# RWKV columns: where a pair's scores and its turned b and k stand, and the row count of two lo products

## The chip, the cores and the metric

The kernel runs on one core of a Trainium2 chip. A core has a matrix engine (TensorE, PE in the profile, with its weight loads as PEld), VectorE (DVE), ScalarE (ACT), GpSimd (POOL), a queue engine that issues transfers (SP), and 16 DMA engines. Each engine executes its own instructions in the order of its program. Matrix products go to PSUM, which has eight banks of 128 x 512 float32. The metric is the time of one execution on the device in microseconds, lower is better.

## The reference, cut to what matters

One decoder layer on a sequence of 1024 tokens with 1024 channels. The part in question is the RWKV-7 branch: 8 heads of 64 channels, whose projections of the normalised input are shifted by one token, turned into decay, rate a, key k, removal vector kk, receptance r and value v, and scanned along the sequence.

```python
p_rwkv = p_rwkv + mu_shift[l] * (prev - p_rwkv)
r, wd, k, v, ad, gd = _split(p, RWKV_COLS)
w = -jax.nn.softplus(-(decay_base + jnp.tanh(wd) @ w_decay_up)) - 0.5
decay = jnp.exp(-jnp.exp(w))
a = jax.nn.sigmoid(iclr_base + ad @ w_iclr_up)
kk = heads(k * kk_scale)                      # then divided by its norm over the head
k = heads(k * (1.0 + (a - 1.0) * k_iclr_mix))
a_vec, b_vec = -kk, kk * a_h
def step(state, inp):                         # 1024 steps
    r_t, w_t, k_t, v_t, a_t, b_t = inp
    sa = jnp.einsum('bhij,bhj->bhi', state, a_t)
    state = state * w_t[:, :, None, :] + sa[..., None] * b_t[:, :, None, :] + v_t[..., None] * k_t[:, :, None, :]
    return state, jnp.einsum('bhij,bhj->bhi', state, r_t)
```

The other branch is forgetting attention (8 heads, softmax with a cumulative bias made from forget gates). Both are merged by gates, projected and added to the residual, and a squared-ReLU MLP follows.

## The kernel before, in words

The scan is done in 16 chunks of 64 tokens. Inside a chunk every pair of tokens needs a score, the product of (kk, r) of one with (b, k) of the other, each scaled by its decay. The stage of the RWKV columns, some 200 us long, makes all of this before the attention and the chunk chain start. It runs over four pairs of heads (`for p in range(4)`, L509), 128 channels per pair on the 128 partitions, tokens along the free axis. For each pair, in the order of writing:

- *Decay and rate* (L511 to L521). Two low-rank products per half of the tokens: p_dec and p_icl, each a product with the high part of the up weights on 128 rows and one with their low part (lo) on 64 rows. The moving operand x2 holds the high part of the 64 inner channels in one half of its rows and the low part in the other, and the weights are loaded twice, one copy in each half. ScalarE makes the tanh (L520, L521). VectorE then makes the step, its running sum (L526), and ScalarE two exponentials ee and ei (L530, L532). wcs (L533) holds a chunk's whole decay.
- *k* (L536 to L552): a projection of 48 matmuls of 128 x 512 (three products of split operands, 8 row blocks, 2 halves), the token shift (`shifted`, L448 on ScalarE and L449 on VectorE), and from it the kk half of the tile ar and both halves of the tile bk, which holds b and k. head_sums (L496) sums kk squared over each head.
- *r* (L555 to L561): projection, shift, the r half of ar (L558), the bonus (L559) and its head sums (tile bo, emptied by ScalarE at L506), the store of ar.
- *v* (L564 to L573): projection, shift, eight transposes (vp) and a store.
- *Scores* (L576 to L586): four groups of four chunks. A group is 16 matmuls on 64 rows each into two PSUM banks, two masked copies on VectorE (COPY_PREDICATED, L585) into one of two score buffers scb, and a 512 KB store to sc_d. The copy must wait until the store of two groups before has landed.
- *Turned b and k* (L589 to L596): one VectorE product of all of bk with wcs, then four times four transposes (bp, L593), a ScalarE copy into one of two staging buffers (tag bt), and a 256 KB store to bk_d.

After the loop come loads of the two sums, the attention's forget-gate bias (`fox_bias`, tile p_f, 32 matmuls and a chain of small VectorE operations), the transposes of those sums, and the gate projection (p_gd). Then the attention starts on TensorE, while GpSimd inverts the chunks' triangular matrices (`inverse`), whose result w_d is read by the chunk chain (`chain`).

What sets the order: the code above gives only data flow and an order of writing. The framework's planner makes each engine's program from it with its own costs for every operation. It takes, among what it holds to be ready, what is written first, so that written-later work fills the waits that it foresees (in the trace matmuls of the next k projection stand between those of v and the scores). On the chip the order is fixed, and an engine waits at its next instruction whatever stands behind it. Small PSUM tiles (`bank`) share four banks, which are handed out in turn; projections (`big`) share two double banks. Most SBUF tiles of the stage have one buffer per name, among them bk, ar, kt and th, so that the next pair's tile needs the last reader of this one. Weights of a projection are loaded two projections ahead on the SP queue, which also issues all stores of the stage.

The functions that the change touches:

Of the kernel before, what the change touches and what calls it, by code (L numbers as in the profile page):

```python
# [8 lines left out]
F32 = mybir.dt.float32  # L9
# [26 lines left out]
def build(ctx, tc, A, out):  # L36
# [3 lines left out]
    def mm(o, l, r, start, stop):  # L40
        PE.matmul(o, l, r, start=start, stop=stop)  # L41
# [24 lines left out]
    def bank(name, tag="ps"):  # L66
        return big(name, tag)
# [96 lines left out]
    def load_w(src, k0, nk, name, to=wp):  # L164

        raw = to.tile([P, nk, P], F32, tag="wraw", name=f"wr_{name}", bufs=2)
        if isinstance(src, (list, tuple)):
            o = 0
            for s_ in src:
                w_ = s_.shape[2]  # L170
                SP.dma_start(raw[:, :, o : o + w_], s_)
                o += w_
        else:
            SP.dma_start(raw, src)
        hi = to.tile([P, nk, P], F32R, tag="whi", name=f"wh_{name}", bufs=2)
        lo = to.tile([P, nk, P], F32R, tag="wlo", name=f"wl_{name}", bufs=2)
        ACT.copy(hi, raw)
        DVE.tensor_tensor(lo, raw, hi.bitcast(F32), ALU.subtract)  # L178
        return hi, lo
# [3 lines left out]
    def win(c0, n=P):  # L183
        return w_in[:, :, c0 : c0 + n]
# [153 lines left out]
    def proj(w, name, ahi=hhi, alo=hlo):  # L338
        hi, lo = w
        o = big(name)  # L340
        for hf in range(2):
            sl = slice(hf * 512, hf * 512 + 512)
            for k in range(KT):
                mm(o[:, sl], hi[:, k, :], ahi[:, k, sl], k == 0, False)
                mm(o[:, sl], lo[:, k, :], ahi[:, k, sl], False, False)
                mm(o[:, sl], hi[:, k, :], alo[:, k, sl], False, k == KT - 1)
        return o
# [111 lines left out]
    with pool(name="ra", bufs=1) as ra:  # L459
# [31 lines left out]
            xs2.append(x2)  # L491

        v4 = lambda ap: ap.rearrange("p (c t) -> p c t", t=C)
        nsc = 0

        def head_sums(a, name, dst, n):  # L496

            hi, lo = [ra.tile([P, S], F32R, name=f"{name}{x}", tag=f"hs{x}") for x in "hl"]
# [7 lines left out]
                ACT.copy(a[0:2, sl], o[0:2])  # L506
            SP.dma_start(dst.rearrange("g h n -> h g n"), a[0:2].rearrange("h (g n) -> h g n", n=n))

        for p in range(4):  # L509

            th = ra.tile([P, S], F32, tag="th", name=f"th{p}")  # L511
            tha = ra.tile([P, S], F32, tag="tha", name=f"tha{p}")
            for hf in range(2):
                sl = slice(hf * 512, hf * 512 + 512)
                od, oi = bank(f"p_dec{p}_{hf}"), bank(f"p_icl{p}_{hf}")
                for i, o in ((0, od), (1, oi)):
                    (hi, lo), me = ups2[i], slice(64 * i, 64 * i + 64)
                    mm(o, hi[:, p * P : (p + 1) * P], xs2[i][:, sl], True, False)
                    mm(o, lo[me, p * P : (p + 1) * P], xs2[i][me, sl], False, True)
                ACT.activation(th[:, sl], od, AF.Tanh, bias=hbase[:, p : p + 1], scale=0.5)  # L520
                ACT.activation(tha[:, sl], oi, AF.Tanh, bias=hbase[:, 4 + p : 5 + p], scale=0.5)  # L521
            stp = step[p % 2]
            DVE.tensor_scalar(stp[:, :, 1:], v4(th), 0.5, 0.5, ALU.mult, ALU.add)
            lc = ra.tile([P, NCH, C + 1], F32, tag="lc", name=f"lc{p}")
            flat = lambda t_: t_.rearrange("p c t -> p (c t)")
            DVE.tensor_tensor_scan(flat(lc), flat(reset), flat(stp), 0.0, ALU.mult, ALU.add)  # L526
            lx = ra.tile([P, NCH, C + 1], F32, tag="lx", name=f"lx{p}")
            DVE.tensor_tensor(lx, lc, lc[:, :, C // 2 : C // 2 + 1].broadcast_to([P, NCH, C + 1]), ALU.subtract)
            ee = ra.tile([P, NCH, C + 1], F32, tag="ee", name=f"ee{p}")
            ACT.activation(ee, lx, AF.Exp, scale=-KAPPA)  # L530
            ei = ra.tile([P, NCH, C + 1], F32, tag="ei", name=f"ei{p}")
            ACT.activation(ei, lx, AF.Exp, scale=KAPPA)  # L532
            DVE.tensor_tensor(wcs[:, p, 0 : NCH - 1].unsqueeze(2), ee[:, 0 : NCH - 1, C : C + 1], ei[:, 1:NCH, 0:1], ALU.mult)  # L533


            o = proj(load_w(win(COL_K + p * P), 0, KT, f"k{p}"), f"p_k{p}") if p else firsts[2][1]  # L536
            kt_ = ra.tile([P, S], F32, tag="kt", name=f"kt{p}")
            shifted(o, 1 + p, kt_)
            ar = ra.tile([P, NCH, P], F32, tag="ar", name=f"ar{p}")
            bk = ra.tile([P, NCH, P], F32, tag="bk", name=f"bk{p}")  # L540
            kks = vcol("kks", p)
            kk2 = ra.tile([P, S], F32, tag="vk", name=f"kk2{p}")
            ACT.activation(kk2, kt_, AF.Square, scale=kks)
            head_sums(kk2, f"sq{p}", sq_d[:, 2 * p : 2 * p + 2], C)
            DVE.scalar_tensor_tensor(ar[:, :, 0:64], v4(kt_), kks, ee[:, :, 0:C], ALU.mult, ALU.mult)
            at = ra.tile([P, S], F32, tag="at", name=f"at{p}")
            (DVE if p else POOL).tensor_scalar(at, tha, 0.5, 0.5, ALU.mult, ALU.add)
            DVE.scalar_tensor_tensor(at, kt_, kks, at, ALU.mult, ALU.mult)
            DVE.tensor_tensor(bk[:, :, 0:64], v4(at), ei[:, :, 1:], ALU.mult)
            (DVE if p else POOL).tensor_scalar(tha, tha, kmh[:, p : p + 1], kmo[:, p : p + 1], ALU.mult, ALU.add)  # L550
            DVE.tensor_tensor(kt_, kt_, tha, ALU.mult)
            DVE.tensor_tensor(bk[:, :, 64:128], v4(kt_), ei[:, :, 1:], ALU.mult)  # L552


            o = proj(load_w(win(COL_R + p * P), 0, KT, f"r{p}"), f"p_r{p}") if p else firsts[1][1]  # L555
            rt = ra.tile([P, S], F32, tag="rt", name=f"rt{p}")
            shifted(o, 5 + p, rt)
            DVE.tensor_tensor(ar[:, :, 64:128], v4(rt), ee[:, :, 1:], ALU.mult)  # L558
            DVE.scalar_tensor_tensor(rt, rt, vcol("rb", p), kt_, ALU.mult, ALU.mult)  # L559
            head_sums(rt, f"bo{p}", bo_d[:, 2 * p : 2 * p + 2], P)  # L560
            SP.dma_start(ar_d.rearrange("c q p n -> q c p n")[:, :, p, :], ar)  # L561


            o = proj(load_w(win(COL_V + p * P), 0, KT, f"v{p}"), f"p_v{p}")  # L564
            vt_ = ra.tile([P, S], F32, tag="vt", name=f"vt{p}")
            shifted(o, 9 + p, vt_)
            vk = ra.tile([P, 8, P], F32, tag="vk", name=f"vk{p}")
            for g in range(2):
                vp = bank(f"vp{p}_{g}")
                for t in range(4):  # L570
                    PE.transpose(vp[:, t * P : (t + 1) * P], vt_[:, (4 * g + t) * P : (4 * g + t + 1) * P], ident)
                ACT.copy(vk[:, 4 * g : 4 * g + 4, :], vp.rearrange("p (t n) -> p t n", n=P))
            SP.dma_start(v_d.rearrange("(t q) n -> q t n", q=P)[:, :, p * P : (p + 1) * P], vk)  # L573


            for g in range(4):  # L576
                sp_ = [bank(f"sc{p}_{g}_{hh}").rearrange("p (c n) -> p c n", c=4) for hh in range(2)]
                for c in range(4):
                    for hh in range(2):
                        hs = slice(64 * hh, 64 * hh + 64)  # L580
                        mm(sp_[hh][:, c, :], bk[hs, 4 * g + c, :], ar[hs, 4 * g + c, :], True, True)
                sb = scb[nsc % 2]
                nsc += 1
                for hh in range(2):
                    DVE.copy_predicated(sb[:, :, hh, :], mask.unsqueeze(1).broadcast_to([P, 4, P]), sp_[hh])  # L585
                SP.dma_start(sc_d[:, 4 * g : 4 * g + 4, p, :], sb.rearrange("p c h n -> p c (h n)"))  # L586


            DVE.tensor_tensor(bk, bk, wcs[:, p, :].unsqueeze(2).broadcast_to([P, NCH, P]), ALU.mult)  # L589
            for g in range(4):  # L590
                bp = bank(f"bp{p}_{g}")
                for c in range(4):
                    PE.transpose(bp[:, c * P : (c + 1) * P], bk[:, 4 * g + c, :], ident)  # L593
                bt = ra.tile([P, 4, P], F32, tag="bt", name=f"bt{p}_{g}", bufs=2)
                ACT.copy(bt, bp.rearrange("p (c n) -> p c n", n=P))
                SP.dma_start(bk_d.rearrange("c q p n -> q c p n")[:, 4 * g : 4 * g + 4, p, :], bt)  # L596

        bol = ra.tile([64, P], F32, name="bol", tag="bt", bufs=2)
        SP.dma_start(nri, sq_d.rearrange("c h s -> (c h) s"))
        SP.dma_start(bol, bo_d.rearrange("t h s -> (t h) s"))  # L600
        fox_bias(ra)
        DVE.tensor_scalar(nri, nri, 1e-24, -1.0, ALU.max, ALU.mult)
        DVE.reciprocal(nri, nri)
        hp = bank("nrp")
# [1053 lines left out]
```

## Time and profile before

| | us |
|---|---|
| median of 3 runs | 1693.91 (1693.02 to 1697.69) |
| profiled execution | 1695.53 |
| its span, first to last instruction | 1693.8 |
| TensorE busy | 1603.3 (95%), mean granted clock 0.988 |
| VectorE, ScalarE, GpSimd busy | 1131.1, 731.3, 359.5 |
| the RWKV columns, from the pairs' first products to the gate projection | about 90 to 289 |

Times in the profile count from the span's start. A matmul's duration is longer than the distance to the next start, since matmuls are pipelined: a stream of 128 x 512 products has 0.39 us each and starts 0.23 us apart. So costs on TensorE are read from the distances between starts. A number in brackets behind a row is the idle time of the engine before it and who ended it. The granted clock is 1.00 at 2.4 GHz and lower in stretches where part of the time ran at 1.2 GHz.

### The profile page before, as it was taken

Reading aid. Unit: us, or ns where it says so; the run is one execution under the profiler, and the core shown is the slowest. Engines: PE = TensorE matmul, PEld = TensorE weight load, DVE = VectorE, ACT = ScalarE, POOL = GpSimd, SP = SyncE. Lnnn points to the kernel's source line nnn. Section 1 sums busy time; section 2 is a strip of 40 time slices with the busy share of each in tenths; the row PEclk is TensorE's granted clock in tenths of the full one; section 3 lists DMA queues with packets and bytes.
Section 4 is the critical chain, followed back from the end, with each engine's and each line's share of the span. In section 5 each row is a group of like instructions: output and inputs, shape, how many; then the busy total and the mean of one; then the engine's idle time right before and its main releaser. Section 6 shows DMA issues by size and latency. Waiting matters only on the chain.

```text
span 1693.8 us, 21902 instructions
## 1 busy us (share of the span) xinstructions
PE 1603.3 (95%) x8293; PEld 1277.2 (75%) x8293; DVE 1131.1 (67%) x1685; ACT 731.3 (43%) x1138; POOL 359.5 (21%) x362
## 2 busy tenths in 40 slices
PE   2999998998999999999999999999999979999997
PEld 2767766776777878888887787777777858888886
DVE  5677665556665736667647655975555579799878
ACT  5454432444454723332233334655555534333334
POOL 4310000699992011121110000112211110000000
PEclk9999999999999999999999999999999989999999
DMA  8534433622223167778768421344444474354422
GB/s 247 140 100 150 127 111 122 155 55 69 61 80 107 44 186 251 224 228 247 230 212 245 171 100 63 131 152 151 146 160 156 164 271 174 124 205 161 157 75 100
DMA packets 217111, 256.24 MB, mean 151 GB/s; under 512 B 30097, under 2 KB 156330, under 8 KB 216878
## 3 DMA queue, kind: packets, MB, share of 16 engines
q1 hardware_dynamic: 204094, 209.99, 40.5%
q0 software_dynamic: 12704, 44.57, 6.9%
q8 instruction: 65, 1.06, 0.3%
q14 instruction: 40, 0.33, 0.1%
q10 hardware_dynamic: 208, 0.28, 0.0%
HBM read 178.16 MB, written 72.45 MB: 148 GB/s over the span
## 4 chain that ended last, share of the span: by engine, by line
PE 71%; DVE 9%; DMA 7%; ACT 3%; issue 2%; SPq 1%; POOL 0%; DVEq 0%; ACTq 0%
PE x L1215 18%; PE y L1215 11%; PE p_out L41 5%; PE p_gb L41 4%; PE p_ga L41 3%; PE p_fk L41 3%; PE p_fq L41 2%; PE my L41 2%; PE p_fv L41 2%; PE p_ob L41 2%; DMA ur<-in_w_ff 2%; PE yv L41 2%; PE p_v L41 2%; PE z L1215 2%; PE p_r L41 2%
## 5 line engine op out<-in xcount | busy, mean ns | idle before, releaser
L1404 ACT CAST dh<-dA 128x1024 fp32r<-128x1024 f32 x54 | 56.4, 1046 | 143.8 <-PE x L1215 74.5
L1215 PE MATMUL x<-wh,dh 128*128 128x512 f32 x256 | 103.7, 405 | 9.4 <-ACT wh L1093 9.4
L1215 PE MATMUL x<-wh,fl 128*128 128x512 f32 x256 | 101.3, 396 | 0.0
L639 POOL TENSOR_TENSOR dg<-dg,inv 128x62 f32<-128x62 f32 (+30 forms) x62 | 100.2, 1615 | 4.8
L1215 PE MATMUL x<-wl,dh 128*128 128x512 f32 x256 | 101.1, 396 | 0.0
L638 POOL TENSOR_TENSOR inv<-dg 128x62 f32<-128x62 f32 (+30 forms) x62 | 92.9, 1498 | 4.9
L1585 DVE TENSOR_TENSOR fl<-dA,dh 128x1024 fp32r<-128x1024 f32 x54 | 65.3, 1218 | 19.4 <-ACT dh L1404 13.1
L1215 PE MATMUL y<-wh,dh 128*128 128x512 f32 x176 | 70.3, 400 | 0.0
L1215 PE MATMUL y<-wl,dh 128*128 128x512 f32 x176 | 68.8, 394 | 0.6 <-DVE wl L1094 0.6
L1215 PE MATMUL y<-wh,fl 128*128 128x512 f32 x176 | 69.2, 393 | 0.0
L823 DVE TENSOR_TENSOR pl<-tp,ph 128x512 fp32r<-128x512 f32 (+1 forms) x80 | 49.1, 631 | 24.7 <-ACT ph L822 24.4
L1215 PEld LDWEIGHTS x<-wh,dh 128*128 128x128 f32 x256 | 48.7, 190 | 20.9 <-ACT wh L1093 9.8
L879 DVE CUSTOM_DVE_ANT_0 pt<-s,cb 128x512 f32<-128x512 f32 (+2 forms) x64 | 36.3, 584 | 37.0 <-PE s L41 36.4
L881 ACT ACTIVATE pt<-pt,sm 128x128 f32<-128x128 f32 (+3 forms) x64 | 49.5, 775 | 25.4 <-DVE sm L879 24.4
L1239 ACT ACTIVATE ff<-ff 128x512 f32<-128x512 f32 x48 | 30.3, 632 | 64.8 <-DVE ff L1325 29.4
L1215 PEld LDWEIGHTS x<-wl,dh 128*128 128x128 f32 x256 | 48.4, 189 | 13.1 <-DVE wl L1094 0.5
L701 POOL TENSOR_TENSOR sw<-sbd,wcs 64x256 f32<-64x256 f32 x28 | 21.9, 782 | 171.3 <-DVE sbd L702 139.3
L1215 PEld LDWEIGHTS x<-wh,fl 128*128 128x128 f32 x256 | 48.6, 190 | 11.4
L822 ACT CAST ph<-tp 128x512 fp32r<-128x512 f32 (+1 forms) x80 | 41.4, 543 | 28.5 <-PE tp L819 26.9
L1230 POOL DMA_DIRECT2D f_d<-ff x48 | 26.0, 542 | 123.5 <-ACT ff L1240 119.0
L41 PE MATMUL p_out<-h_wo,hhi 128*128 128x512 f32 x128 | 50.8, 396 | 1.1 <-ACT h_wo L1050 1.1
L41 PE MATMUL p_gb<-hhi,wl_gb 128*128 128x512 f32 x128 | 51.5, 402 | 0.2 <-DVE wl_gb L178 0.2
(586 smaller groups left out, 4938.1 us busy)
## 6 DMA issues: line engine op xcount, KB each, us to landing
dA<-f_d SPq DMA_DIRECT2D x27, 1024.0 KB
aw<-in_w_ada SPq DMA_DIRECT2D x32, 512.0 KB
ur<-in_w_ff SPq DMA_DIRECT2D x30, 512.0 KB
B<-in_w_ff SPq DMA_DIRECT2D x15, 1024.0 KB
f_d<-ff POOLq DMA_DIRECT2D x48, 256.0 KB, 4.4
wa<-in_w_ada SPq DMA_DIRECT2D x16, 512.0 KB
sc_d<-scb SPq DMA_DIRECT2D x16, 512.0 KB
sct<-sc_d SPq DMA_DIRECT2D x16, 512.0 KB
```

Source lines behind the costliest of these rows:

```text
L41: PE.matmul(o, l, r, start=start, stop=stop)
L638: POOL.tensor_tensor(tv, dg[:, 0:s, s : s + 1].broadcast_to([P, s, m]), dg[:, s : s + 1, s + 1 :].broadcast_to([P, s, m]), ALU.mult)
L639: POOL.tensor_tensor(dg[:, 0:s, s + 1 :], dg[:, 0:s, s + 1 :], tv, ALU.add)
L822: ACT.copy(ph[:, 0:w_], tp[:, 0:w_])
L823: DVE.tensor_tensor(pl[:, 0:w_], tp[:, 0:w_], ph[:, 0:w_].bitcast(F32), ALU.subtract)
L879: DVE.tensor_tensor_reduce(pt[:, c0:c1], sv, cb[:, c0:c1], -0.125, low, ALU.add, ALU.min, st_[:, x : x + 1])
L881: ACT.activation(pt[:, 0:n], pt[:, 0:n], AF.Exp, bias=low, scale=-1.0, accum_out=ls[:, b : b + 1])
L1215: PE.matmul(o, l, r, start=start, stop=stop, skip_group_check=True)
L1230: POOL.dma_start(f_d[AOPS.index(name), j], src)
L1239: ACT.activation(f, f, AF.Relu)
L1404: ACT.copy(hs[i], src[:, 2 * i : 2 * i + 2])
L1585: DVE.tensor_tensor(fl[:, sl], src[:, sl], f32(hs[i_]), ALU.subtract)
```

## The change

The loop body of scores becomes a function `scores(p, bk, ar, gs)` and the turning of b and k a function `leave(p, bk)`. Groups 0 and 1 of a pair's scores are now written ahead of v's projection, groups 2 and 3 where all four were. The turning of a pair's b and k is written behind the next pair's k projection, and for the last pair behind `fox_bias`. The lo products of decay and rate run on all 128 rows of weights and x2; this adds the product of the low weights with the low part of x.

```diff
--- before.py
+++ after.py
@@ -491,8 +491,6 @@
             xs2.append(x2)
 
         v4 = lambda ap: ap.rearrange("p (c t) -> p c t", t=C)
-        nsc = 0
-
         def head_sums(a, name, dst, n):
 
             hi, lo = [ra.tile([P, S], F32R, name=f"{name}{x}", tag=f"hs{x}") for x in "hl"]
@@ -506,6 +504,30 @@
                 ACT.copy(a[0:2, sl], o[0:2])
             SP.dma_start(dst.rearrange("g h n -> h g n"), a[0:2].rearrange("h (g n) -> h g n", n=n))
 
+        def scores(p, bk, ar, gs):
+
+            for g in gs:
+                sp_ = [bank(f"sc{p}_{g}_{hh}").rearrange("p (c n) -> p c n", c=4) for hh in range(2)]
+                for c in range(4):
+                    for hh in range(2):
+                        hs = slice(64 * hh, 64 * hh + 64)
+                        mm(sp_[hh][:, c, :], bk[hs, 4 * g + c, :], ar[hs, 4 * g + c, :], True, True)
+                sb = scb[g % 2]
+                for hh in range(2):
+                    DVE.copy_predicated(sb[:, :, hh, :], mask.unsqueeze(1).broadcast_to([P, 4, P]), sp_[hh])
+                SP.dma_start(sc_d[:, 4 * g : 4 * g + 4, p, :], sb.rearrange("p c h n -> p c (h n)"))
+
+        def leave(p, bk):
+
+            DVE.tensor_tensor(bk, bk, wcs[:, p, :].unsqueeze(2).broadcast_to([P, NCH, P]), ALU.mult)
+            for g in range(4):
+                bp = bank(f"bp{p}_{g}")
+                for c in range(4):
+                    PE.transpose(bp[:, c * P : (c + 1) * P], bk[:, 4 * g + c, :], ident)
+                bt = ra.tile([P, 4, P], F32, tag="bt", name=f"bt{p}_{g}", bufs=2)
+                ACT.copy(bt, bp.rearrange("p (c n) -> p c n", n=P))
+                SP.dma_start(bk_d.rearrange("c q p n -> q c p n")[:, 4 * g : 4 * g + 4, p, :], bt)
+
         for p in range(4):
 
             th = ra.tile([P, S], F32, tag="th", name=f"th{p}")
@@ -514,9 +536,9 @@
                 sl = slice(hf * 512, hf * 512 + 512)
                 od, oi = bank(f"p_dec{p}_{hf}"), bank(f"p_icl{p}_{hf}")
                 for i, o in ((0, od), (1, oi)):
-                    (hi, lo), me = ups2[i], slice(64 * i, 64 * i + 64)
+                    hi, lo = ups2[i]
                     mm(o, hi[:, p * P : (p + 1) * P], xs2[i][:, sl], True, False)
-                    mm(o, lo[me, p * P : (p + 1) * P], xs2[i][me, sl], False, True)
+                    mm(o, lo[:, p * P : (p + 1) * P], xs2[i][:, sl], False, True)
                 ACT.activation(th[:, sl], od, AF.Tanh, bias=hbase[:, p : p + 1], scale=0.5)
                 ACT.activation(tha[:, sl], oi, AF.Tanh, bias=hbase[:, 4 + p : 5 + p], scale=0.5)
             stp = step[p % 2]
@@ -534,6 +556,8 @@
 
 
             o = proj(load_w(win(COL_K + p * P), 0, KT, f"k{p}"), f"p_k{p}") if p else firsts[2][1]
+            if p:
+                leave(p - 1, bk)
             kt_ = ra.tile([P, S], F32, tag="kt", name=f"kt{p}")
             shifted(o, 1 + p, kt_)
             ar = ra.tile([P, NCH, P], F32, tag="ar", name=f"ar{p}")
@@ -560,6 +584,8 @@
             head_sums(rt, f"bo{p}", bo_d[:, 2 * p : 2 * p + 2], P)
             SP.dma_start(ar_d.rearrange("c q p n -> q c p n")[:, :, p, :], ar)
 
+            scores(p, bk, ar, (0, 1))
+
 
             o = proj(load_w(win(COL_V + p * P), 0, KT, f"v{p}"), f"p_v{p}")
             vt_ = ra.tile([P, S], F32, tag="vt", name=f"vt{p}")
@@ -572,33 +598,13 @@
                 ACT.copy(vk[:, 4 * g : 4 * g + 4, :], vp.rearrange("p (t n) -> p t n", n=P))
             SP.dma_start(v_d.rearrange("(t q) n -> q t n", q=P)[:, :, p * P : (p + 1) * P], vk)
 
-
-            for g in range(4):
-                sp_ = [bank(f"sc{p}_{g}_{hh}").rearrange("p (c n) -> p c n", c=4) for hh in range(2)]
-                for c in range(4):
-                    for hh in range(2):
-                        hs = slice(64 * hh, 64 * hh + 64)
-                        mm(sp_[hh][:, c, :], bk[hs, 4 * g + c, :], ar[hs, 4 * g + c, :], True, True)
-                sb = scb[nsc % 2]
-                nsc += 1
-                for hh in range(2):
-                    DVE.copy_predicated(sb[:, :, hh, :], mask.unsqueeze(1).broadcast_to([P, 4, P]), sp_[hh])
-                SP.dma_start(sc_d[:, 4 * g : 4 * g + 4, p, :], sb.rearrange("p c h n -> p c (h n)"))
-
-
-            DVE.tensor_tensor(bk, bk, wcs[:, p, :].unsqueeze(2).broadcast_to([P, NCH, P]), ALU.mult)
-            for g in range(4):
-                bp = bank(f"bp{p}_{g}")
-                for c in range(4):
-                    PE.transpose(bp[:, c * P : (c + 1) * P], bk[:, 4 * g + c, :], ident)
-                bt = ra.tile([P, 4, P], F32, tag="bt", name=f"bt{p}_{g}", bufs=2)
-                ACT.copy(bt, bp.rearrange("p (c n) -> p c n", n=P))
-                SP.dma_start(bk_d.rearrange("c q p n -> q c p n")[:, 4 * g : 4 * g + 4, p, :], bt)
+            scores(p, bk, ar, (2, 3))
 
         bol = ra.tile([64, P], F32, name="bol", tag="bt", bufs=2)
         SP.dma_start(nri, sq_d.rearrange("c h s -> (c h) s"))
         SP.dma_start(bol, bo_d.rearrange("t h s -> (t h) s"))
         fox_bias(ra)
+        leave(3, bk)
         DVE.tensor_scalar(nri, nri, 1e-24, -1.0, ALU.max, ALU.mult)
         DVE.reciprocal(nri, nri)
         hp = bank("nrp")
```

## Rows read from the trace of the kernel before

**Rows 1.** Engine totals on the page's first part: busy us, share, instructions.

```profile
PE 1603.3 (95%) x8293; PEld 1277.2 (75%) x8293; DVE 1131.1 (67%) x1685; ACT 731.3 (43%) x1138; POOL 359.5 (21%) x362
```

**Rows 2.** Windows by pair: length, busy us per engine (instructions), PEclk, DMA share, GB/s.

```profile
126.00:169.00 43.00, 40.24 (x232) 31.05 (x232) 32.02 (x33) 17.91 (x25) 0.00 (x0) 1.00 0.50 153
169.00:221.00 52.00, 47.65 (x251) 36.85 (x249) 30.87 (x30) 19.18 (x25) 0.00 (x0) 0.97 0.42 127
221.00:273.00 52.00, 47.59 (x249) 34.76 (x249) 31.38 (x32) 19.19 (x25) 0.00 (x0) 0.95 0.40 124
273.00:290.00 17.00, 16.60 (x75) 12.00 (x74) 7.26 (x34) 3.70 (x8) 0.00 (x0) 0.94 0.25 79
```

**Rows 3.** TensorE's waits from 90 to 290: total us, times, longest.

```profile
PE bp L593 <- DVE bk L589: 11.7, 4, 4.2
```

**Rows 4.** Chain of waits in pair 3: start us, us, what.

```profile
253.35 2.78 PE p_f L41 x12
...
257.01 1.14 PE sc L41 x16
...
259.50 6.08 DMA sc_d<-scb
...
267.02 2.18 DVE bk L589
```

**Rows 5.** Timeline of TensorE, b and k transposes: start us, us, instruction [idle before].

```profile
126.38 1.99 PE L593 MATMUL bp<-ident,bk 128*128 128x128 f32 x16 [1.09 <-DVE bk L589]
...
167.19 1.99 PE L593 MATMUL bp<-ident,bk 128*128 128x128 f32 x16 [2.20 <-DVE bk L589]
...
217.37 3.41 PE L593 MATMUL bp<-ident,bk 128*128 128x128 f32 x16 [4.18 <-DVE bk L589]
...
269.25 3.67 PE L593 MATMUL bp<-ident,bk 128*128 128x128 f32 x16 [4.23 <-DVE bk L589]
272.58 0.78 PE L41 MATMUL p_f<-hlo,wfs 128*16 128x512 f32 x1
...
275.15 0.39 PE L41 MATMUL p_f<-hlo,wfs 128*16 128x512 f32 x1
```

**Rows 6.** Timeline of TensorE, decay and rate products of pair 1.

```profile
128.12 0.48 PE L41 MATMUL p_dec<-x,h_w_decay_up 128*128 128x512 f32 x1
...
129.83 0.50 PE L41 MATMUL p_r<-hlo,wh_r 128*128 128x512 f32 x1
130.17 0.40 PE L41 MATMUL p_r<-hhi,wh_r 128*128 128x512 f32 x1
130.40 0.39 PE L41 MATMUL p_dec<-x,h_w_decay_up 128*128 128x512 f32 x1
```

**Rows 7.** Timeline of TensorE behind the scores of pair 1.

```profile
161.03 0.50 PE L41 MATMUL p_k<-hhi,wl_k 128*128 128x512 f32 x1
161.37 0.40 PE L41 MATMUL p_k<-hlo,wh_k 128*128 128x512 f32 x1
```

**Rows 8.** Timeline of VectorE in pair 3.

```profile
224.38 0.70 DVE L523 TENSOR_SCALAR step<-th 128x1024 f32<-128x1024 f32 x1 [5.82 <-ACT th L520]
...
239.19 1.22 DVE L552 TENSOR_TENSOR bk<-kt,ei 128x1024 f32<-128x1024 f32 x1
...
244.92 1.22 DVE L558 TENSOR_TENSOR ar<-rt,ee 128x1024 f32<-128x1024 f32 x1
```

**Rows 9.** Timeline of ScalarE in pairs 0 and 3.

```profile
97.25 0.69 ACT L521 ACTIVATE tha<-p_icl,hbase 128x512 f32<-128x512 f32 x1 [0.16 <-PE p_icl L41]
...
241.44 1.12 ACT L448 ACTIVATE rt<-p_r,omu 128x1024 f32<-128x1024 f32 x1 [2.83 <-PE p_r L41]
...
250.43 1.05 ACT L506 COPY rt<-bo 2x512 f32<-2x512 f32 x2 [1.88 <-PE bo L41]
```

**Rows 10.** The tensor w_d: instructions, duration ns min/median/max, first and last start us.

```profile
L661 SPq DMA_DIRECT2D wt<-w_d x16: 605/611/898, 603.2 to 830.8; - x16
L643 POOL DMA_DIRECT2D w_d<-dg x1: 746/746/746, 520.1 to 520.1; - x1
```

## Prediction

> **What bounds the kernel now.** I read the busy shares first. TensorE is busy for 1603 us, 95% of the span [rows 1], so a change pays if it removes TensorE work or TensorE idle time. The windows over the pairs come next [rows 2]: pair 1's ends with TensorE busy 40.24 us of 43.00, those of pairs 2 and 3 with 47.65 and 47.59 of 52.00. The reader should see that some 4.4 us in each of the later two are idle, and that the granted clock is below 1.00 there (0.97 and 0.95). The list of TensorE's waits gives the idle time one owner: the transposes of b and k (bp, L593) wait 11.7 us in four times for VectorE's product with wcs (bk, L589) [rows 3].
>
> Who makes that product late is told by the chain of waits of pair 3 [rows 4]: first scores, then 6.08 us until a 512 KB store of scores (sc_d) lands, then the product, then the transposes. The four groups of a pair follow each other at once, there are two score buffers, so group 2's masked copy cannot start until group 0's store has landed, and the product stands behind that copy on VectorE. The same rows tell how TensorE's order is made: 12 matmuls of p_f, written after the scores, run ahead of them (2.78 us at 253.35). The planner lets ready work overtake, but it put the transposes 4 us too early for what the store really took, and p_k or p_f work that was ready stood behind them.
>
> The idle times before the transposes are 1.09, 2.20, 4.18 and 4.23 us [rows 5]. After the last two TensorE restarts at the lower of its two levels: the 16 transposes take 3.41 and 3.67 us where they took 1.99 in pairs 0 and 1.
>
> **The change part by part.** All terms are set against the profiled execution, 1695.53 us (span 1693.8 and 1.73 around it), which is 1.62 us above the median of the three runs, 1693.91.
>
> *Half the scores ahead of v.* Per pair 32 of 64 score matmuls, 4 masked copies and 2 stores move to before v's projection. They cannot run right there: ar is ready at 244.92 + 1.22 = 246.1 [rows 8], 4.7 us after r's projection ended (its shift starts at 241.44 [rows 9]). So I expect them inside v's projection, group 0 some 5 to 8 us into it, group 1 near its end, because its PSUM banks are those of the bonus sums, which ScalarE empties by 250.43 + 1.05 = 251.5 [rows 9]. Between group 0's store and group 2's copy then lie the rest of v (48 starts of 0.23 us from 241.4 on reach past 252), the shift and v's transposes, an estimated 8 us, against a landing time of 6.08 [rows 4]. In pairs 1 to 3 the wait goes. In pair 0 v's projection ran early, before the scores' inputs existed, so nothing separates the halves and I keep its 1.09 us. What becomes late next in the other pairs is group 3's copy, waiting for group 1's store; it holds up only two banks of the next decay products, and k's projection is there to fill.
>
> *Turning b and k behind the next k projection.* One VectorE product of 2.27 us, 16 transposes, 4 ScalarE copies and 4 stores (SP queue) move behind 48 matmuls. The product gets some 10 us of cover, in a stretch where VectorE stood idle 5.82 us before the step operation [rows 8]; if that cover failed it would cost its 2.3 us per pair. The copies come to ScalarE beside kt's shift; the next pair's b and k are written by 239.19 + 1.22 = 240.4, 5.7 us before ar [rows 8], which is the slack that they may eat. On SP the stores go after the loads of the next weights, which then wait less. The last pair's share moves behind the forget-gate bias, and there its staging buffer (tag bt, two of them) is shared with bol, and its banks come after those of the bias: its copies and stores run one after another into the gate projection. I price that at 0, with an upper bound of one store landing, 6.1 us [rows 4]. Removed idle time by the two edits together: 2.20 + 4.18 + 4.23 = 10.6 us [rows 5], bounds 6.4 (one pair keeps its wait) and 11.7 [rows 3].
>
> *The clock.* Without those gaps no restart at the low level: 3.41 - 1.99 = 1.4 us, 3.67 - 1.99 = 1.7 us, and six starts of p_f from 272.58 to 275.15 in 2.57 us where six at the steady 0.23 us are 1.4, so 1.2 us more. Sum 4.3 us [rows 5], bound below 1.4 us, if pair 3's gap stays.
>
> *Lo products on all rows.* Before, the lo product of decay and of rate uses 64 rows of the array, between products on 128. From 128.12 to 130.40 six starts take 2.28 us, where six at 0.23 us would be 1.38: 0.90 us for two such products, 0.45 each [rows 6]. On all rows this goes; no instruction is added. Pairs 1 to 3 have 12: 5.4 us. In pair 0 the tanh waits only 0.16 us for TensorE [rows 9], so I take 0.2 of its 1.8. Sum 5.6 us, bounds 5.4 and 7.2.
>
> A rule of the Trainium skill speaks against this term: the page "TensorE: Matmul & The Clock Gate", section "Why this matters for your kernels", says that a single small-K matmul takes the same time as one of K = 128. By it alone the edit would be worth nothing and the sum 11.3 us. The rows put the price on the starts behind each change of the row count; to that the Trainium skill's page "TensorEngine Tiling (Array Packing)", section "Key Properties", has that a change of tiling mode drains the engine, and gives no price.
>
> *What the split of the scores costs.* The scores use 64 rows too, in one run per pair. The way out of it shows the same step: from 161.03 to 161.37 is 0.34 instead of 0.23 [rows 7]. Cut into pieces, each further piece costs one way in and out, 0.45 us by [rows 6]. Two pieces more per pair (group 0, group 1, then 2 and 3 together) are 8 x 0.45 = 3.6 us; bounds 1.8 (one more) and 5.4 (three more).
>
> Sum: 10.6 + 4.3 + 5.6 - 3.6 = 16.9 us. The stretch behind is TensorE's too, and its other long worker has room: w_d is issued at 520.1 and first read at 603.2 [rows 10], so GpSimd's inverse does not hold the gain back, and I pass it on whole. 1695.5 - 16.9 = 1678.6 for a profiled execution, and 1.6 less, 1677.0, as a median.
>
> **The rivals.**
>
> *The scores park TensorE inside v's projection.* If the planner puts the moved scores too early, v's ready matmuls stand behind them as p_k's and p_f's stood behind the transposes. At the head of v's projection the first group would wait 4.7 us for ar and the second until the bonus sums are emptied, 10.0 us after r's end (251.5 - 241.44) [rows 8, 9]. Three pairs of that are 30 us, and the clock's 4.3 us comes back: 1677 + 30 + 4 = 1711. It decides from 16.9 / 3 = 5.6 us of such waiting per pair. Against it: the planner already places the bonus sums, which depend on the same ar and rt operations, inside v's projection with no wait in TensorE's list, and it misjudged the store, not VectorE. Chance 0.06.
>
> *The store's wait only changes its owner.* If group 1 runs no sooner than v's end, group 3 and the next decay products wait for the banks as the transposes did, and the idle time and the clock stay. Left are 5.6 - 3.6 = 2.0 us: 1691.9, no change. For it: the landing time of 6 us is near the 8 us I count between the halves. Against it: group 0's buffer is free in any case, and half of the wait would be gone. Chance 0.09.
>
> *The last pair's tail shows.* The late copies hold ScalarE, or SP behind their stores, at the head of the attention stage, for one landing: 1677.0 + 6.1 = 1683.1. Chance 0.15.
>
> *The lo products are worth nothing.* The slow starts then come from something else in that spot, such as the tanh emptying the banks on ScalarE, and stay with 128 rows: 1677.0 + 5.6 = 1682.6. Against it: the same step stands behind the scores, where no bank is short [rows 7]. Chance 0.05. This is also the result by the Trainium skill's page "TensorE: Matmul & The Clock Gate", section "Why this matters for your kernels".
>
> **How the numbers follow.** The forecast has 0.65, so 1677.0 is the prediction. The best bounds are 11.7 + 4.3 + 7.2 - 1.8 = 21.4 us: 1672.5. The worst that I still hold the same case is 6.4 + 1.4 + 5.4 - 5.4 = 7.8 less the tail of 6.1, so 1.7 us, 1692; both at once are unlikely. The range 1672 to 1691 holds the forecast and the two smaller gains. About 0.3%, 5.1 us, is what a measurement of this kernel can tell from no change. Faster by more: 0.65 + 0.15 + 0.05 = 0.85. Within: 0.09. Slower: 0.06.
>
> **What would show it.** In the profile after, the transposes should have no wait in TensorE's list, VectorE's masked copies almost none for sc_d in pairs 1 to 3, the 16 transposes should take about 2 us everywhere, and the clock should stay at 1.00 up to the attention stage. Around p_dec the starts should be 0.23 apart. Score matmuls should stand in two or three runs per pair, the first inside p_v without a wait. I am wrong if sc, p_dec or p_v appears in TensorE's list of waits with more than 2 us per pair, or if the stretch shrinks by 15 us and the end does not follow.

## The result and the profile after

The kernel after takes 1679.13 us (median of 4 runs, 1675.93 to 1682.71) against 1694.22 us before in the same comparison; the ratio is 0.9897, with a 95% interval of 0.9868 to 0.9926. The forecast was 1677.0 in a range of 1672 to 1691. The profiled execution took 1680.21 us, with a span of 1678.5.

The engine totals on the first part of the page after answer to [rows 1]:

```profile
PE 1591.5 (95%) x8293; PEld 1274.8 (76%) x8293; DVE 1132.0 (67%) x1685; ACT 730.7 (44%) x1138; POOL 357.9 (21%) x362
```

TensorE executes as many matmuls as before and is busy 11.8 us less. Its list of waits from 80 to 300 us in the kernel after (columns: total us, times, longest) answers to [rows 3]:

```profile
PE p_k L41 <- DVE wl_k L178: 3.8, 1, 3.8
PE p_dec L41 <- DVE scb L517: 1.2, 2, 0.6
PE sq L41 <- DVE sq1l L498: 0.8, 1, 0.8
PE p_dec L41 <- DVE x L490: 0.7, 1, 0.7
PE sq L41 <- ACT sq3h L497: 0.6, 1, 0.6
PE sq L41 <- ACT sq2h L497: 0.6, 1, 0.6
```

The 11.7 us of the transposes are gone. What is new are small waits for head sums (sq), 1.2 us of p_dec in pair 0, and a longer wait for the low half of k's second weights, wl_k. Before, that wait was

```profile
PE p_k L41 <- DVE wl_k L178: 2.0, 1, 2.0
```

VectorE's wait for the landing of score stores, from which the transposes' wait came, was 13.7 us before and is 0.6 after (first line before, second after):

```profile
DVE scb L585 <- DMA sc_d<-scb: 13.7, 3, 5.0
```

```profile
DVE scb L517 <- DMA sc_d<-scb: 0.6, 1, 0.6
```

The windows by pair after (length, busy us per engine with instructions, PEclk, DMA share, GB/s), to be held against [rows 2]:

```profile
125.00:165.00 40.00, 38.38 (x218) 29.59 (x219) 31.00 (x32) 19.07 (x25) 0.00 (x0) 1.00 0.50 152
165.00:210.50 45.50, 44.90 (x249) 35.20 (x249) 30.71 (x31) 18.85 (x25) 0.00 (x0) 1.00 0.46 139
210.50:256.00 45.50, 44.88 (x251) 34.22 (x250) 31.18 (x33) 18.83 (x25) 0.00 (x0) 1.00 0.47 141
256.00:276.00 20.00, 19.56 (x102) 13.98 (x101) 11.19 (x38) 2.96 (x7) 0.00 (x0) 1.00 0.34 111
```

Pairs 2 and 3 go from 52 us each to 45.5, TensorE is busy all but 0.6 us in them, and the granted clock is 1.00. The timeline of TensorE after shows the moved parts in place (start, duration, instruction):

```profile
210.47 0.50 PE L41 MATMUL p_dec<-x,h_w_decay_up 128*128 128x512 f32 x1
210.81 0.40 PE L41 MATMUL p_dec<-x,l_w_decay_up 128*128 128x512 f32 x1
211.08 0.50 PE L41 MATMUL p_icl<-x,h_w_iclr_up 128*128 128x512 f32 x1
211.42 0.40 PE L41 MATMUL p_icl<-x,l_w_iclr_up 128*128 128x512 f32 x1
...
212.27 0.39 PE L41 MATMUL p_icl<-x,h_w_iclr_up 128*128 128x512 f32 x1
212.50 0.39 PE L41 MATMUL p_icl<-x,l_w_iclr_up 128*128 128x512 f32 x1
...
220.92 1.91 PE L526 MATMUL bp<-ident,bk 128*128 128x128 f32 x16
...
243.61 0.72 PE L41 MATMUL sc<-ar,bk 64*128 64x128 f32 x8
244.31 0.62 PE L41 MATMUL bo<-bo3l,selr 128*2 128x512 f32 x2
244.86 2.13 PE L41 MATMUL sc<-ar,bk 64*128 64x128 f32 x24
...
253.98 2.06 PE L41 MATMUL sc<-ar,bk 64*128 64x128 f32 x32
```

The last products of decay and rate start 0.23 us apart where [rows 6] has 0.43 (the first ones, behind the scores, are still 0.27 to 0.34 us apart although the row count stays at 128 between them; no run shows why); the transposes take 1.91 us without a wait where [rows 5] has 3.41 and 3.67; and the scores of pairs 1 to 3 stand in three pieces (8, 24 and 32), the first two inside v's projection. On VectorE the masked copies of the second half follow 10 us behind the first, so their buffers are free:

```profile
245.61 2.56 DVE L517 COPY_PREDICATED scb<-mask,sc 128x512 f32<-128x512 uint8 x4 [1.35 <-PE sc L41]
...
255.17 2.57 DVE L517 COPY_PREDICATED scb<-mask,sc 128x512 f32<-128x512 uint8 x4 [1.18 <-PE sc L41]
257.64 2.27 DVE L522 TENSOR_TENSOR bk<-bk,wcs 128x2048 f32<-128x2048 f32 x1
```

For the experiments I use one measure, called the stage: from the last start of p_wa to the first start of p_fv on TensorE. In windows with these ends the kernels before and after stand as follows (columns as above):

```profile
82.58:288.88 206.30, 190.59 (x1005) 143.07 (x1004) 133.96 (x163) 83.95 (x114) 7.47 (x2) 0.98 0.40 121
```

```profile
83.47:275.88 192.41, 183.98 (x1006) 140.37 (x1005) 135.35 (x163) 82.28 (x112) 5.20 (x2) 0.99 0.41 125
```

The stage is 13.9 us shorter; the two executions' spans differ by 15.3. The other 1.4 us are 2.3 won behind the stage less 0.9 lost ahead of it, where the change edits nothing. Adding up the distances from each start to the next by tile within the stage gives where the 13.9 us came from:

| TensorE in the stage, us | before | after | difference |
|---|---|---|---|
| waiting | 15.7 | 8.4 | -7.3 |
| transposes of b and k, without waits | 10.0 | 6.7 | -3.2 |
| p_f, without waits | 8.8 | 7.4 | -1.4 |
| decay and rate products, without waits | 13.1 | 9.0 | -4.0 |
| scores, bonus sums, v's transposes, without waits | 26.6 | 27.7 | +1.1 |
| k's projections, without waits | 35.8 | 36.2 | +0.4 |
| all else | | | +0.5 |

### The profile page after: what moved, and what is told of

The parts are those of the page before. It is cut to its first block, busy times and chain, and to the rows that moved or that the text cites. A ratio compares the mean times of both kernels' runs of the same rounds, so it can differ in the third digit from the quotient of the medians.

```text
span 1678.5 us, 21911 instructions
## 1 busy us (share of the span) xinstructions
PE 1591.5 (95%) x8293; PEld 1274.8 (76%) x8293; DVE 1132.0 (67%) x1685; ACT 730.7 (44%) x1138; POOL 357.9 (21%) x362
## 4 chain that ended last, share of the span: by engine, by line
PE 70%; DVE 10%; DMA 7%; ACT 5%; issue 3%; SPq 0%; DVEq 0%; ACTq 0%
PE x L1221 18%; PE y L1221 11%; PE p_gb L41 5%; PE p_out L41 5%; PE p_ga L41 3%; PE p_ob L41 2%; PE p_fv L41 2%; DMA ur<-in_w_ff 2%; PE my L41 2%; PE p_fk L41 2%; PE p_fq L41 2%; PE z L1221 2%; PE p_v L41 2%; PE yv L41 2%; PE tp L825 2%
## 5 line engine op out<-in xcount | busy, mean ns | idle before, releaser
L825 PE MATMUL tp<-ident,pt 128*128 128x128 f32 x288 | 49.6, 282 | 2.1 <-ACT pt L887 1.7
```

Of the source, the lines that this page charges most:

```text
L825: PE.transpose(tp[:, x * P : (x + 1) * P], pr[b][:, t * P : (t + 1) * P], ident)
```

## The experiments

Theory: the transposes waited because VectorE could not reuse a score buffer whose store had not landed, and the split of the scores, the turning and the lo products each bring their term. The main rival: the wait only changes its owner. All eight combinations of the three edits were run (before and after among them), then kernels that act on the suspected buffer and on pair 0's wait. The stage of one kernel repeats within about 1 us (after: 192.4 and 193.4 in two profiles). What lies behind the stage took 1398 to 1406 us over all profiles, though the instructions there are the same kind and number, so a stage gain of 2 or 3 us can't be told from medians.

**Lo products alone.**

```diff
-                    (hi, lo), me = ups2[i], slice(64 * i, 64 * i + 64)
+                    hi, lo = ups2[i]
-                    mm(o, lo[me, p * P : (p + 1) * P], xs2[i][me, sl], False, True)
+                    mm(o, lo[:, p * P : (p + 1) * P], xs2[i][:, sl], False, True)
```

> The kernel before with the lo products of decay and rate on all 128 rows and nothing else; every engine keeps its order of instructions. Stage = first start of p_fv minus last start of p_wa on TensorE: 206.3 us before, 192.4 after the whole change. Theory A (the price is in the steps between 64 and 128 rows, 0.45 us each): decay and rate products fall from 13.05 us to about 9.0, the stage by 4 to 5.4 us, the median by as much. Theory B (a single 64-row product costs what a 128-row one costs, the slow starts come from something else): the stage stays within 1 us of 206.3.

Measured: ratio 0.9979 (0.9960 to 0.9998). Decay and rate products fell from 13.05 to 9.21 us, as Theory A has it, but the stage only from 206.3 to 205.5: the price of the row counts is real and did not reach the end. Where most of it went is seen in pair 0. VectorE and GpSimd there in the kernel before (start, duration, instruction):

```profile
98.03 3.05 POOL L547 TENSOR_SCALAR at<-tha 128x1024 f32<-128x1024 f32 x1 [17.67 <-ACT tha L521]
...
97.91 2.33 DVE L526 TENSOR_TENSOR_SCAN lc<-reset,step 128x1040 f32<-128x1040 f32 x1
...
102.32 1.23 DVE L528 TENSOR_TENSOR lx<-lc 128x1040 f32<-128x1040 f32 x1
```

and with the lo products alone:

```profile
97.93 1.05 POOL L547 TENSOR_SCALAR at<-tha 128x1024 f32<-128x1024 f32 x1 [17.25 <-ACT tha L521]
99.09 4.15 POOL L550 TENSOR_SCALAR tha<-tha,kmh,kmo 128x1024 f32<-128x1024 f32 x1
...
98.09 3.07 DVE L526 TENSOR_TENSOR_SCAN lc<-reset,step 128x1040 f32<-128x1040 f32 x1
...
102.25 2.07 DVE L528 TENSOR_TENSOR lx<-lc 128x1040 f32<-128x1040 f32 x1
```

The faster products give the rate's tanh sooner, GpSimd starts 0.16 us ahead of VectorE's running sum instead of 0.12 behind it, and now VectorE is the one that loses: 3.07 instead of 2.33 us, and 2.07 instead of 1.23 for lx (which overlaps GpSimd's next operation until 103.24), 1.6 us together. The low half of k's weights (wl_k) stands behind both. Counted from the stage's start it is made only 0.4 us later, because a wait of VectorE for GpSimd, 0.9 us before, is gone; but the faster products bring TensorE there 1.4 us sooner. So TensorE's wait for wl_k grows from 2.0 to 3.9 us: it takes back what pair 0's products had saved, and more. Behind it k's products start 0.43 us apart from 107.0 to 110.4, a restart at the lower clock that costs some 1.6 us and that the profile before doesn't have. A new wait for head sums takes 1.2 us more.

**The split alone, and the turning alone.** The first calls `leave(p, bk)` right behind the last scores, the second calls scores for all four groups behind v; both keep the lo products on 64 rows.

```diff
-            if p:
-                leave(p - 1, bk)
...
             scores(p, bk, ar, (2, 3))
+            leave(p, bk)
```

> The kernel before with groups 0 and 1 of the scores written ahead of v's projection and nothing else: b and k are still turned right behind the scores, lo products on 64 rows. Theory A (the transposes waited for the landing of the score stores, and the distance between the halves alone removes that wait): the waits of the transposes fall from 11.7 us to under 4, no lower clock, stage 206.3 - 10 to - 13 us. Theory B (the distance is not enough, turning behind k's projection is what takes the wait off TensorE): the transposes still wait more than 7 us in all, stage less than 5 us shorter. Each further piece of scores costs 0.45 us by the forecast, 3.6 us in all; if the pieces cost nothing the stage is 4 us shorter than A's.

```diff
-            scores(p, bk, ar, (0, 1))
...
-            scores(p, bk, ar, (2, 3))
+            scores(p, bk, ar, (0, 1, 2, 3))
```

> The kernel before with b and k turned behind the next k projection and nothing else: four groups of scores in a row, lo products on 64 rows. Theory A (k's projection is cover enough): VectorE still waits some 5 us per pair for sc_d, TensorE no longer does, stage 206.3 - 11 to - 15 us. Theory B (the wait changes its owner: the next decay products need the banks that the late copies hold): p_dec waits 2 to 4 us per pair in TensorE's list, stage less than 6 us shorter.

Measured: the split alone has a ratio of 0.9888 (0.9857 to 0.9919) and a stage of 194.4 us, the turning alone 1.0035 (1.0015 to 1.0055) and 210.0. With the split the transposes wait 1.9 us in all. With the turning alone the wait changes its owner, as the rival said; the chain of waits of that kernel in pair 2:

```profile
211.97 5.07 DMA sc_d<-scb
...
217.16 0.73 DVE scb L517
...
217.94 1.52 PE p_dec L41 x2
```

The next decay products need the PSUM banks of group 2, whose copy waits for the store. TensorE's list has p_dec for 6.8 us in place of the transposes' 11.7, so 4.9 us were covered (a product of the forget-gate bias now waits 2.2 us, 1.8 more than before), but the stage's mean clock fell, and with it more was lost:

```profile
82.11:292.10 209.99, 197.43 (x1006) 146.07 (x1004) 134.07 (x163) 83.19 (x112) 7.47 (x2) 0.93 0.38 115
```

That is a granted clock of 0.93 where the kernel before has 0.98. Without waits, the decay and rate products take 16.3 us of starts instead of 13.1 and k's projections 42.4 instead of 35.8. In pair 2 the lower clock lasts from the wait's end at 217.9 to 229.4, and then the starts are 0.23 us apart again:

```profile
226.03 0.63 PE L41 MATMUL p_k<-hhi,wh_k 128*128 128x512 f32 x1
226.45 0.63 PE L41 MATMUL p_k<-hhi,wl_k 128*128 128x512 f32 x1
...
229.83 0.39 PE L41 MATMUL p_k<-hhi,wh_k 128*128 128x512 f32 x1
230.06 0.39 PE L41 MATMUL p_k<-hhi,wl_k 128*128 128x512 f32 x1
```

In the kernel before the lower clock ended with the transposes in pair 2 and after six starts of p_f behind them in pair 3 [rows 5]. That the transposes, work between the wait and the decay products, shorten the slow stretch isn't shown: with three score buffers (below) they stand there in pair 1, from 169.8 to 172.0, and the starts behind them are slow until 180.9.

**One edit taken back.** The kernel after without the turning, without the lo products, and without the split, by the diffs above.

> The kernel after with b and k turned right behind the scores again (split scores and lo products on all rows stay). Stage as before (206.3 us before, 192.4 after, 194.4 with the split alone). Theory A (with the split the product is in time, and turning behind k's projection adds only the rest of the transposes' wait, 1.9 us with the split alone): stage 192.4 + 0 to 2, time within 0.2% of the kernel after. Theory B (the move carries a third or more of the gain once the split is in): stage 197 us or more.

> The kernel after with the lo products on 64 rows again. Theory A (their price is real TensorE time and TensorE bounds the stage): stage 192.4 + 3.4 to 4 = 196 us. Theory B (as in the kernel before, where the edit alone moved the stage by 0.8 us, most of it comes back as waits for k's low weights and a restart at the lower clock in pair 0): stage 192.4 + 0 to 1.5.

> The kernel after with all four groups of scores behind v's projection again (turning behind k and lo products on all rows stay). Theory A (the split is what takes the wait away; without it the decay products wait for the banks that the late copies hold, as with the turning moved alone, 209.99 us): p_dec waits 5 to 8 us in TensorE's list, stage 204 to 208 us, no faster than before. Theory B (lo products and turning together make up for it): stage under 200 us.

Measured: without the turning 0.9892 (0.9854 to 0.9929), stage 192.6; without the lo products 0.9942 (0.9916 to 0.9969), stage 196.6; without the split 0.9999 (0.9976 to 1.0023), stage 204.3 and p_dec waiting 7.8 us. Theory A holds for all three (without the lo products the loss is 4.2 us, a little over its 3.4 to 4). The eight stages in us:

| | neither | turning | split | both |
|---|---|---|---|---|
| lo on 64 rows | 206.3 | 210.0 | 194.4 | 196.6 |
| lo on 128 rows | 205.5 | 204.3 | 192.6 | 192.4 |

So the split carries the gain (11.9 us alone, 11.9 of 13.9 when taken from the whole). The turning costs 2.2 and 3.7 us where the lo products are on 64 rows; where they are on 128 it gives 1.2 without the split and 0.2 with it, against the 1 us by which two profiles of one kernel differ. So in the whole change these runs show no gain of the turning.

**More score buffers.** Three, with one step buffer to make room:

```diff
-        step = [ra.tile([P, NCH, C + 1], F32, name=f"step{i}") for i in range(2)]
-        scb = [ra.tile([P, 4, 2, P], F32, name=f"scb{i}") for i in range(2)]
+        step = [ra.tile([P, NCH, C + 1], F32, name=f"step{i}") for i in range(1)]
+        scb = [ra.tile([P, 4, 2, P], F32, name=f"scb{i}") for i in range(3)]
-                sb = scb[nsc % 2]
+                sb = scb[nsc % 3]
```

> The kernel before with three score buffers in place of two (and one step buffer in place of two, to make room) and no other edit. Theory A (the wait is for a buffer whose store has not landed): with a third buffer group 2 need not wait, the waits of the transposes fall from 11.7 us to under 5, the restarts at the lower clock go, stage 206.3 - 8 to - 15 us. Theory B (VectorE's own work or the banks make the product late): the waits stay above 9 us and the stage within 3 us of 206.3.

Then four, with lx in the space of th besides:

```diff
-            lx = ra.tile([P, NCH, C + 1], F32, tag="lx", name=f"lx{p}")
+            lx = ra.tile([P, NCH, C + 1], F32, tag="th", name=f"lx{p}")
```

> The kernel before with four score buffers in place of two, so that no masked copy of a pair waits for a store of the same pair; to make room one step buffer in place of two, and the tile lx in the space of th. Nothing else is edited. Theory A (the transposes waited for the landing of this pair's score stores): VectorE's waits for sc_d and TensorE's for the product fall under 2 us in all, stage 206.3 - 10 to - 13 us, the same gain as the split alone (194.4). Theory B (the product was late for another reason, as three buffers, which left 10.4 us, could suggest): waits of the transposes above 8 us, stage over 202.

Measured with three: ratio 0.9979 (0.9958 to 1.0000), stage 208.3, the transposes still waiting 10.4 us; taken by its numbers, that run went against the theory. Its timeline of VectorE in pair 2 shows why:

```profile
212.85 3.78 DVE L585 COPY_PREDICATED scb<-mask,sc 128x512 f32<-128x512 uint8 x6 [1.14 <-PE sc L41]
220.31 1.33 DVE L585 COPY_PREDICATED scb<-mask,sc 128x512 f32<-128x512 uint8 x2 [3.69 <-DMA sc_d<-scb]
221.54 2.27 DVE L589 TENSOR_TENSOR bk<-bk,wcs 128x2048 f32<-128x2048 f32 x1
```

Group 2 copies at once, group 3 now waits for group 0's landing, and the product with wcs stands behind group 3. With four buffers, in the same pair:

```profile
204.04 5.01 DVE L585 COPY_PREDICATED scb<-mask,sc 128x512 f32<-128x512 uint8 x8 [1.14 <-PE sc L41]
208.93 2.28 DVE L589 TENSOR_TENSOR bk<-bk,wcs 128x2048 f32<-128x2048 f32 x1
```

Eight copies in a row, the product directly behind them, no wait of the transposes at all, a stage of 191.6 us and a ratio of 0.9910 (0.9891 to 0.9929). That is the gain of the split with no score moved, and it shows the landing of a pair's own stores as the cause.

**Pair 0's wait for wl_k.** In the kernel after:

```diff
+            if p == 0:
+                wv0 = load_w(win(COL_V), 0, KT, "v0")
+                wk1 = load_w(win(COL_K + P), 0, KT, "k1")
             stp = step[p % 2]
```

(v's first and k's second projection then use these.)

> The kernel after with the weight loads and splits of v's first and k's second projection written ahead of pair 0's decay step, so that VectorE makes the low half of k's weights before the running sum. Theory A (TensorE's 3.8 us wait for wl_k in pair 0, and the 3.4 us at the lower clock behind it, are on the path): the wait goes from TensorE's list, stage 192.4 - 3 to - 5.5 us, 1673.5 to 1676 us. Theory B (pair 0's own chain on VectorE is the bound, and 1.2 us ahead of it come back later): stage within 1 us of 192.4.

Measured: the wait is gone, stage 187.3 us, as Theory A has it, but the ratio is 0.9891 (0.9857 to 0.9925), no better than the kernel after. Behind the stage that profile took 1406.1 us, 3.5 more than the kernel after; 2.7 of them lie in the attention's first operands up to the last p_fq, with a granted clock of 0.91 in one 20 us window:

```profile
290.00:310.00 20.00, 18.00 (x77) 14.04 (x77) 9.81 (x12) 5.29 (x10) 17.24 (x16) 0.91 0.56 155
```

The corresponding window of the kernel after has 1.00:

```profile
296.00:316.00 20.00, 17.62 (x84) 13.79 (x84) 11.35 (x17) 7.07 (x15) 17.46 (x16) 1.00 0.56 151
```

Both have the same wait in it (p_fq for kl, 2.0 us). The fall is not tied to the early weights: from the first p_fv to the last p_fq ten of the fourteen profiles take 267.9 to 268.5 us and four 270.6 to 271.1 (early weights, no lo products, no split, and the last combination below), each of the four with a granted clock of 0.91 there, while the split combination, early weights included, has 1.00. Why the clock fell in the one and not in the other stays open.

**The kernel after again, and combinations.** The second is the split with lo products and early weights, turning as before the change; the third, compared with the kernel before alone, is the kernel before with four buffers, lo products and early weights.

> The kernel after, unchanged, beside the next two on one chip, so that they are compared under the same conditions. Stage from p_wa's last to p_fv's first start 192.4 us in its first profile: if stages repeat, within 0.5 us of that; if the clock's restarts differ from execution to execution, within 2 us. Median near 0.990 of the kernel before.

> Split scores, lo products on all rows and the early low half of k's second weights, with b and k turned right behind the scores as in the kernel before. Theory A (the turning's place carries nothing once the halves are apart; the early weights take 5 us off the stage): stage 192.6 - 5 = 187 to 188 us, median 0.3% under the kernel after where no restart at the lower clock behind the stage takes it back. Theory B (turning behind k's projection is needed to keep the 5 us): stage 190 us or more.

> The kernel before with four score buffers (191.56 us of stage by themselves), lo products on all rows, and the early low half of k's second weights; scores and turning stand as in the kernel before. Theory A (the three savings lie on different waits and add): stage 191.6 - 4 - 4 = 183 to 185 us, median 8 us under the kernel after's ratio, 0.985 to 0.988 of the kernel before. Theory B (beyond some point the shortest path through VectorE and the head sums takes back what TensorE saves): stage 187 us or more, waits for sq and bo in TensorE's list over 4 us.

Measured: the kernel after 0.9904 (0.9885 to 0.9923), stage 193.4 (the 1.0 us against its first profile is pair 0's stretch at the lower clock, thirteen slow starts instead of seven); the split combination 0.9898 (0.9872 to 0.9925), stage 189.0; the four-buffer combination 0.9882 (0.9858 to 0.9905), median 1676.55 us, stage 187.9. The two stages are above what the sums of their parts gave (187 to 188 and 183 to 185). The split combination lies between its two theories; the four-buffer one has waits of 3.7 us for head sums sq and 0.7 for bo, so its Theory B holds. The four-buffer combination has the lowest ratio of all and beats the kernel before clearly; against the kernel after the intervals overlap, so that it beats both isn't shown.

## Why the prediction was right, step by step

*What bounds the kernel* was right: TensorE's stage, the product with wcs, and the store's landing behind it; four buffers show it directly.

*The idle time.* Forecast 10.6 us, measured 7.3. Every wait of the transposes went, pair 0's too, and 0.7 us of the scores' own. The step mis-sized is what comes in its place: 1.2 us of p_dec in pair 0, where the halves are not apart, 2.0 of head sums and 1.8 more of wl_k. The forecast named the banks of the decay products as next in line and gave them nothing.

*"Removed idle time by the two edits together"* is where the attribution was loose. The split does it alone. Of the turning the forecast said that k's projection is cover enough; alone it made the kernel slower, by the mechanism of the rival "the store's wait only changes its owner". That rival was tied to the wrong edit: it is what the turning does without the split.

*The clock.* Forecast 4.3 us. The transposes and p_f gave 4.6, but behind pair 0's wait for wl_k a restart came that the profile before doesn't have: k's projections have 36.2 us of starts in the kernel after and 34.7 with the early weights, whose stage has a clock of 1.00. Net about 3. That the longer wait brought it isn't shown: with the split alone and with four buffers the wait is 2.0 and 2.1 us, as before the change, and the same restart follows.

*Lo products.* Forecast 5.6 us, of which 0.2 for pair 0; measured 4.0 in TensorE's own time against the kernel before, and between kernels that have the split and differ in the lo products alone 4.5 without the turning (12.96 to 8.50) and 5.0 with it (14.0 to 9.0). The price per product was close. The step that failed is pair 0's, which had 0.2 us and nothing as its lower bound: it came out negative, because TensorE's next product there starts 22.6 us from the stage's start instead of 22.2, behind the stretched work of VectorE. The rule of the Trainium skill by which the edit is worth nothing ("TensorE: Matmul & The Clock Gate", section "Why this matters for your kernels") does not hold for a product between products of another row count; the trace agrees with the drain of the Trainium skill's "TensorEngine Tiling (Array Packing)", section "Key Properties", and puts 0.2 us on each change of mode.

*The split's cost.* Forecast 3.6 us for two pieces more per pair, measured 1.1 with exactly these two. The last 32 scores of a pair take 1.98 us from their first start to the next product, where all 64 took 4.88 before [rows 7 has their end]: the run of 64 itself waited for banks that copies had to empty. In the kernel before the weight loads of the scores wait for those copies,

```profile
PEld sc L41 <- DVE scb L585: 2.2, 8, 0.3
```

and the list after has no such line. That saving was not in the sum.

*The tail of the last pair* was priced at 0, and is: its transposes ran from 272.45 inside p_gd, the four stores took SP 5.84 us from 273.70, TensorE is busy 19.56 of 20.00 us there, and the stretch behind up to the last p_fq takes 268.2 us where it took 267.9. *Scores parked inside v's projection*, the slower rival, did not come: no wait for ar in the list.

*The sum.* Forecast 16.9 us less, measured 15.1 between the medians. That it came so near is in part luck: idle time, clock and lo products gave 3.3, about 1 and 1.6 us less than forecast, the pieces of the scores cost 2.5 us less, and the 1.4 us that the profiled execution won outside the stage were in no term.

## What to carry to other kernels

When a store frees the buffer of the next group, look for distance between the groups before hiding the consumer behind other work: here distance took 11.9 us off the stage and two more buffers 14.7, while hiding alone moved the wait to the next reader of the same banks and lost 3.7. Test a buffer theory with enough buffers for the whole burst, since one buffer more only moves the wait to the next group. And an edit that makes TensorE faster ahead of a chain on VectorE and GpSimd can change which of the two starts first, so its gain must be read at the end of the stage and not in its own instructions.

## What was not expected of the hardware

Whether VectorE's running sum (two SBUF inputs) or GpSimd's tensor_scalar starts first decides which of them is stretched: 2.33 and 3.05 us with VectorE first, 3.07 and 1.05 with GpSimd first. All four kernels with the lo products and the old place of the weights (after, alone, without turning, without split) have VectorE's 135.3 to 135.5 us and GpSimd's 5.20 in the stage, all with lo on 64 rows 133.4 to 134.2 and 7.46 or 7.47; the wait for wl_k is 3.8 to 3.9 us in the first and 2.0 to 2.1 in the second (in this difference the faster products, which bring TensorE there sooner, have the larger part). This agrees with the Trainium skill's page "SBUF — State Buffer", section "SBUF: two separate sides": the two engines share a port pair as a lock, whoever starts first keeps it for the whole instruction, and the other blocks.
